# Attention outputs of a two-layer hybrid decoder as float32r products of split values and split, already divided probabilities, on one Trainium2 core

## Chip, cores and metric

One core of a Trainium2 chip (trn2) runs the whole kernel in one launch. The metric is the device time of an execution in microseconds, as the median of three runs. PE is TensorE, DVE is VectorE, ACT is ScalarE, POOL is GpSimd, SP is SyncE, which issues nearly all DMAs.

## What is computed

Two layers, each a half-step SwiGLU, a token-mixing sub-layer and another half-step SwiGLU, all on 512 tokens of width 1024, in float32. The mixing has three parts side by side: forgetting attention (4 heads of 64), dilated attention (4 heads of 64) and an HGRN2 recurrence (4 heads of 128). The part at hand is the two attentions:

```
def _fox_attention(q, k, v, c):
...
        s = jnp.einsum('bhqd,bhkd->bhqk', qi, k).astype(jnp.float32) * scale
        s = s + ci[..., None] - c[:, :, None, :]
...
        p = jax.nn.softmax(jnp.where(mask, s, NEG_BIG), axis=-1)
        return jnp.einsum('bhqk,bhkd->bhqd', p.astype(v.dtype), v)
...
def _dilated_attention(q, k, v):
    outs, lses = [], []
    for window, dilation in DILATED_PATTERNS:
        o, lse = _dilated_branch(q, k, v, window, dilation)
        outs.append(o)
        lses.append(lse)
    wts = jax.nn.softmax(jnp.stack(lses, 0), axis=0)
    return jnp.sum(wts[..., None] * jnp.stack(outs, 0), axis=0)
...
    o = jnp.concatenate([oa.astype(h.dtype), ob.astype(h.dtype), oc.astype(h.dtype)], axis=-1)
    return o @ w_out
```

The kernel computes the three dilated patterns as one softmax: the logarithm of the number of patterns that hold a pair of positions is added to its score by a mask. The sum over the patterns weighted by their denominators is just that softmax.

## The kernel before

Activations stand transposed, as [column, token], in eight blocks of 128 columns by 512 tokens. Large products run in float32r, one pass over PE, on operands that are split in two: a float32r high part that ACT casts (L269 for the weights) and the low part, which DVE gets by subtraction (L271). A product is then three matmuls, high by high, high by low and low by high (mm3, L274 to L278). Weights come by DMA in 512 KB pieces, three ahead (L266).

`ffn` and the closures of `mixing` are written as plain loops. The instructions of each engine stand in an order that the build decides from dependencies and priorities: `load_split` raises the priority of the weights' splits by 400 places (AHEAD), `run` that of the chains of the mixing by 100 (CHAIN). At run time each engine takes its list in that order.

In `mixing` come, for each layer: the HGRN heads (`decays`, `states`), the dilated attention, the forgetting attention, and `gated`, which projects the gate (`proj_t("HG")`, into hg_ps), applies a sigmoid (L840), multiplies the HGRN outputs by it and transposes them. While that goes on, `first_rows` starts the output projection (o_ps). `add_rows` takes the row blocks in the order f, d, h: two of forgetting attention (ohf and olf, the high and low parts of its transposed output), two of dilated (ohd, old), four of HGRN.

`attend` (L637 to L673) does both attentions, for four blocks of 128 queries (b) and four heads (h). For one head and n = 128(b + 1) keys:

- PE writes the scores into the one bank sc (L647), from float32r operands.
- DVE adds the mask and takes the minimum of the negated scores, into neg and nm (L651).
- ACT takes the exponential in place and sums it into den (L655).
- PE transposes the 128x128 pieces into the one bank pt (L659).
- ACT, for odd heads, or DVE, for even heads, copies them to pt in memory (L662, L664).
- PE multiplies in plain float32, the transposed probabilities being the stationary operand and the 64 columns of values the moving one (L666), into po as [query, column]:

```
                        PE.matmul(po[:, h * HD:(h + 1) * HD], pt[:, j * 128:(j + 1) * 128],
                                  val[:, j, h * HD:(h + 1) * HD], start=j == 0, stop=j == b)
```

Behind the four heads DVE divides by den (L669 and L671, into o), and `put_out` transposes the two pieces of o on PE (L537), ACT casts the high part (L542), and DVE subtracts for the low one (L543). The values vv are one plain float32 tile of [128, 4, 512], which ACT writes out of v_ps (L724).

Of the kernel before, what the change touches and what calls it, by code (L numbers as in the profile page):

```python
# [19 lines left out]
HD = 64  # L20
# [109 lines left out]
def hybrid_trunk(ctx: ExitStack, tc: tile.TileContext, a, out):  # L130
# [355 lines left out]
    def mixing(l, after, r, rb):  # L486
# [150 lines left out]
        def attend(kind, operands, val, mask):  # L637

            for b in range(NB):
                n = (b + 1) * 128  # L640
                den = lines(mp, [128, 4], tag="den", name="den", bufs=2)
                po = gen("po", "po")
                for h in range(4):
                    ps = gen("sc", "sc_ps")
                    terms = operands(h)
                    for i, (q, k) in enumerate(terms):
                        PE.matmul(ps[:, 0:n], q[:, b * 128:(b + 1) * 128], k[:, 0:n],  # L647
                                  start=i == 0, stop=i == len(terms) - 1)
                    neg = mp.tile([128, T], F32, tag="neg", name="neg", bufs=3)
                    nm = lines(mp, [128, 1], tag="nm", name="nm", bufs=2)  # L650
                    V.tensor_tensor_reduce(out=neg[:, 0:n], in0=ps[:, 0:n], in1=mask[:, 512 - n:512],  # L651
                                           scale=-1.0, scalar=3.0e38, op0=ALU.add, op1=ALU.min,
                                           accum_out=nm)
                    pr = neg
                    S.activation(pr[:, 0:n], neg[:, 0:n], AF.Exp, bias=nm, scale=-1.0,  # L655
                                 accum_out=den[:, h:h + 1])
                    pt_ps = gen("pt", "pt_ps")
                    for j in range(b + 1):
                        PE.transpose(pt_ps[:, j * 128:(j + 1) * 128], pr[:, j * 128:(j + 1) * 128], ident)  # L659
                    pt = mp.tile([128, T], F32, tag="pt", name="pt", bufs=2)  # L660
                    if h % 2:
                        S.copy(pt[:, 0:n], pt_ps[:, 0:n])  # L662
                    else:
                        V.tensor_copy(pt[:, 0:n], pt_ps[:, 0:n])  # L664
                    for j in range(b + 1):
                        PE.matmul(po[:, h * HD:(h + 1) * HD], pt[:, j * 128:(j + 1) * 128],  # L666
                                  val[:, j, h * HD:(h + 1) * HD], start=j == 0, stop=j == b)
                    yield
                V.reciprocal(den, den)  # L669
                o = mp.tile([128, 4, HD], F32, tag="o4", name="o4", bufs=1)  # L670
                V.tensor_tensor(out=o, in0=po[:, 0:256].rearrange("p (h d) -> p h d", h=4),  # L671
                                in1=den.unsqueeze(2).to_broadcast([128, 4, HD]), op=ALU.mult)
                put_out(kind, b, o.rearrange("p h d -> p (h d)"), 2)  # L673


        vv = slot("VV", (128, NB, 512), "vv")


        def dilated():
# [41 lines left out]
                                               op0=ALU.mult, op1=ALU.subtract)  # L721
            pss = proj_t("V", "v_ps")
            for b in range(NB):
                S.activation(vv[:, b, :], pss[b], AF.Copy, scale=r[:, b:b + 1])  # L724
            dv = vv[:, :, 0:256]
            def operands(h):
                i, n = divmod(h, 2)
                return [(q2[i][:, n, :], kh[i][:, n, :]), (q2[i][:, n, :], kl[i][:, n, :])]
# [20 lines left out]
            return ch, cl  # L749

        def forgetting(ch, cl):
            fv = vv[:, :, 256:512]


            q2 = [pair(t, f"fq{t}", R32) for t in ("A2", "A6")]
            k2 = [pair(t, f"fk{t}", R32) for t in ("V0", "V1")]
            qc = [pair(t, f"fqc{t}", R32) for t in ("am", "F0")]
            kc = [pair(t, f"fkc{t}", R32) for t in ("F1",)]
            kc.append(slot("ob", (128, 3, T), "fkcob", R32)[:, 0:2, :])
            for i in range(2):  # L760
                G.memset(qc[i][64:68].bitcast(F32), -1.0)
                G.memset(kc[i][64:68].bitcast(F32), 1.0)
                for n in range(2):
                    h = 2 * i + n
                    for part, c in enumerate((ch, cl)):
                        nc.sync.dma_start(out=qc[i][66 + part:67 + part, n, :].bitcast(F32), in_=c[h:h + 1, :].bitcast(F32))
                        nc.sync.dma_start(out=kc[i][64 + part:65 + part, n, :].bitcast(F32), in_=c[h:h + 1, :].bitcast(F32))
                ps = proj_d(f"FQ{i}", "fq_ps")
                u = mp.tile([128, 768], F32, tag="qk", name="fu", bufs=2)[:, 0:T]
                V.scalar_tensor_tensor(out=u, in0=ps, scalar=0.125, in1=rb, op0=ALU.mult, op1=ALU.mult)  # L770
                for n in range(2):
                    own, other = slice(64 * n, 64 * n + 64), slice(64 - 64 * n, 128 - 64 * n)
                    S.copy(q2[i][own, n, :], u[own])
                    S.copy(qc[i][0:64, n, :], u[own])
                    V.tensor_tensor(out=q2[i][other, n, :], in0=u[own], in1=q2[i][own, n, :].bitcast(F32),
                                    op=ALU.subtract)
                ps = proj_d(f"FK{i}", "fk_ps")
                u = mp.tile([128, 768], F32, tag="qk", name="fu", bufs=2)[:, 0:T]
                V.tensor_tensor(out=u, in0=ps, in1=rb, op=ALU.mult)
                for n in range(2):  # L780
                    own, other = slice(64 * n, 64 * n + 64), slice(64 - 64 * n, 128 - 64 * n)
                    S.copy(k2[i][own, n, :], u[own])
                    S.copy(k2[i][other, n, :], u[own])
                    V.tensor_tensor(out=kc[i][0:64, n, :], in0=u[own], in1=k2[i][own, n, :].bitcast(F32),
                                    op=ALU.subtract)
            def operands(h):
                i, n = divmod(h, 2)
                return [(q2[i][:, n, :], k2[i][:, n, :]), (qc[i][0:68, n, :], kc[i][0:68, n, :])]

            return attend("f", operands, fv, masks[:, 0, :])  # L790


# [78 lines left out]
        def add_rows(half, pair):  # L871
            wh, wl = load_split(a["w_out"][l, half, pair], KB, 128)
            for i in range(2):
                d = 2 * pair + i
                if not half:
                    pss[d] = acc("o_ps")
                for j in range(4):
                    k = 4 * half + j
                    kind, n = rows[k]
                    mm3(pss[d], wh[:, 4 * i + j, :], wl[:, 4 * i + j, :], oth[kind][n // 2][:, n % 2, :],  # L880
                        otl[kind][n // 2][:, n % 2, :], k == 0, k == KB - 1)
                if half:
                    V.tensor_tensor(out=x[d], in0=pss[d], in1=x[d], op=ALU.add)
                    after(d)
                yield
# [53 lines left out]
```

## Time and profile before

| | us |
|---|---|
| median of three runs | 2067.0 (2066.81 to 2067.48) |
| profiled execution | 2066.05 |
| its span, from the first to the last instruction | 2064.3 |
| PE busy | 2043.4 (99%) |
| DVE busy | 1025.8 (50%) |
| ACT busy | 731.6 (35%) |
| granted TensorE clock, mean | 0.999 |

PE is occupied throughout. Its matmuls are pipelined, so the duration of one (0.39 us for 512 columns) is longer than the step from one to the next. A plain float32 matmul leaves two records, a float32r matmul and a transpose one. The attention stands in two stretches, at 511 to 621 us and, for the second layer, about 1562 to 1641 us.

### The profile page before, as it was taken

How to read it: one execution, taken by the hardware profiler on the slowest of the kernel's cores; microseconds unless marked ns; L12 is line 12 of the kernel's file. 1: busy time of each engine (PE TensorE's matmuls, PEld its weight loads, DVE VectorE, ACT ScalarE, POOL GpSimd, SP SyncE). 2: the span in 40 equal slices, each digit the busy share in tenths (PEclk: the TensorE clock that was granted, in tenths of full speed). 3: DMA queues.
4: the chain of work that ended last, by engine and by line, in shares of the span. 5: the costliest groups of instructions: out<-in, count | busy, mean ns of one | idle time of the engine just before them, and what ended most of it. 6: DMA issues, size and time to landing. Idle time of an engine off the chain costs nothing.

```text
span 2064.3 us, 23885 instructions
## 1 busy us (share of the span) xinstructions
PE 2043.4 (99%) x9636; PEld 1685.6 (82%) x9636; DVE 1025.8 (50%) x1636; ACT 731.6 (35%) x1104; POOL 12.8 (1%) x18
## 2 busy tenths in 40 slices
PE   8999999999999999999999999999999999999998
PEld 6888888888788888888888888888888888888886
DVE  8544433556656644443354444336566565444333
ACT  5332322433654323232232322233346443232222
POOL 0000000000000000000000000000000000000000
PEclk9999999999999999999999999999999999999999
DMA  4323233211212232333323233332112122323222
GB/s 169 97 97 100 91 95 104 93 52 61 67 42 92 92 96 98 98 92 98 101 92 102 92 102 94 95 97 82 62 42 77 52 92 93 102 92 102 97 97 82
DMA packets 54310, 184.91 MB, mean 90 GB/s; under 512 B 7336, under 2 KB 7464, under 8 KB 54200
## 3 DMA queue, kind: packets, MB, share of 16 engines
q1 hardware_dynamic: 53592, 182.28, 27.6%
q8 instruction: 75, 1.23, 0.2%
q10 hardware_dynamic: 576, 1.05, 0.1%
q14 instruction: 35, 0.29, 0.0%
q0 software_dynamic: 32, 0.07, 0.0%
HBM read 181.21 MB, written 2.10 MB: 89 GB/s over the span
## 4 chain that ended last, share of the span: by engine, by line
PE 95%; DVE 2%; ACT 1%; issue 1%; DMA 0%; SPq 0%; DVEq 0%; ACTq 0%
PE gu_ps L278 15%; PE gu_ps L277 15%; PE gu_ps L276 15%; PE d_ps L276 6%; PE d_ps L278 6%; PE d_ps L277 6%; PE d_ps L451 5%; PE lv_ps L593 2%; PE po L666 2%; PE o_ps L278 1%; PE o_ps L276 1%; PE o_ps L277 1%; PE sc_ps L647 1%; PE pt_ps L659 1%; PE hg_ps L517 1%; PE hg_ps L518 1%
## 5 line engine op out<-in xcount | busy, mean ns | idle before, releaser
L269 ACT CAST wh<-raw 128x1024 fp32r<-128x1024 f32 (+1 forms) x344 | 357.2, 1039 | 1053.9 <-issue 407.8
L271 DVE TENSOR_TENSOR wl<-raw,wh 128x1024 fp32r<-128x1024 f32 (+1 forms) x344 | 414.2, 1205 | 300.4 <-ACT wh L269 298.4
L276 PE MATMUL gu_ps<-xh,wh 128*128 128x512 f32 x1408 | 548.6, 390 | 6.6 <-ACT wh L269 6.6
L278 PE MATMUL gu_ps<-xh,wl 128*128 128x512 f32 x1408 | 548.8, 390 | 0.2
L277 PE MATMUL gu_ps<-xl,wh 128*128 128x512 f32 x1408 | 548.2, 389 | 0.0
L276 PEld LDWEIGHTS gu_ps<-xh,wh 128*128 128x128 f32 x1408 | 264.7, 188 | 61.6 <-ACT wh L269 6.6
L278 PEld LDWEIGHTS gu_ps<-xh,wl 128*128 128x128 f32 x1408 | 264.6, 188 | 56.2 <-DVE wl L271 1.3
L277 PEld LDWEIGHTS gu_ps<-xl,wh 128*128 128x128 f32 x1408 | 264.7, 188 | 55.2 <-DVE xl L190 0.2
L276 PE MATMUL d_ps<-hh,wh 128*128 128x512 f32 x528 | 205.4, 389 | 0.0
L277 PE MATMUL d_ps<-hl,wh 128*128 128x512 f32 x528 | 205.4, 389 | 0.0
L278 PE MATMUL d_ps<-hh,wl 128*128 128x512 f32 x528 | 205.4, 389 | 0.0
L406 DVE TENSOR_TENSOR u<-gu_ps,rb 128x512 f32<-128x512 f32 x88 | 60.8, 691 | 265.1 <-PE gu_ps L278 264.9
L403 DVE TENSOR_TENSOR g<-gu_ps,rb 128x512 f32<-128x512 f32 x88 | 60.8, 691 | 172.9 <-PE gu_ps L278 172.7
L278 PEld LDWEIGHTS d_ps<-hh,wl 128*128 128x128 f32 x528 | 99.1, 188 | 20.6
L277 PEld LDWEIGHTS d_ps<-hl,wh 128*128 128x128 f32 x528 | 99.1, 188 | 20.6
L276 PEld LDWEIGHTS d_ps<-hh,wh 128*128 128x128 f32 x528 | 99.1, 188 | 20.5
L409 ACT CAST hh<-u 128x512 fp32r<-128x512 f32 x88 | 55.1, 626 | 57.5 <-DVE u L407 57.5
L451 PE MATMUL d_ps<-wl,hh 128*128 128x512 f32 x176 | 69.0, 392 | 0.3 <-DVE wl L271 0.3
L451 PE MATMUL d_ps<-wh,hl 128*128 128x512 f32 x176 | 68.8, 391 | 0.0
L451 PE MATMUL d_ps<-wh,hh 128*128 128x512 f32 x176 | 68.4, 392 | 0.0
L407 DVE TENSOR_TENSOR u<-u,g 128x512 f32<-128x512 f32 x88 | 60.9, 692 | 8.1
L593 PEld LDWEIGHTS lv_ps<-hQ,hk 128*128 128x128 f32 x448 | 55.7, 191 | 8.4 <-issue 6.1
(292 smaller groups left out, 2403.3 us busy)
## 6 DMA issues: line engine op xcount, KB each, us to landing
raw<-in_ffn_w_gate SPq DMA_DIRECT2D x88, 512.0 KB, 3.4
raw<-in_ffn_w_up SPq DMA_DIRECT2D x88, 512.0 KB, 3.4
raw<-in_w_in SPq DMA_DIRECT2D x58, 512.0 KB, 3.4
raw<-in_ffn_w_down SPq DMA_DIRECT2D x48, 448.0 KB, 3.3
raw<-in_ffn_w_down SPq DMA_DIRECT2D x24, 512.0 KB, 3.5
raw<-in_last_w_down SPq DMA_DIRECT2D x22, 512.0 KB, 3.5
raw<-in_w_out SPq DMA_DIRECT2D x16, 512.0 KB, 3.4
x<-in_x SPq DMA_DIRECT2D x8, 256.0 KB, 5.4
```

What stands on the lines that cost most here:

```text
L269: S.copy(wh, raw)
L271: V.tensor_tensor(out=wl, in0=raw, in1=wh.bitcast(F32), op=ALU.subtract)
L276: PE.matmul(ps, lh, rh, start=first, stop=False)
L277: PE.matmul(ps, lh, rl, start=False, stop=False)
L278: PE.matmul(ps, ll, rh, start=False, stop=last)
L403: V.tensor_tensor(out=g, in0=part[0], in1=rb, op=ALU.mult)
L406: V.tensor_tensor(out=u, in0=part[1], in1=rb, op=ALU.mult)
L407: V.tensor_tensor(out=u, in0=u, in1=g, op=ALU.mult)
L409: S.copy(h1, u)
L451: PE.matmul(ps, h[:, s], w, start=first and n == 0, stop=last and n == len(terms) - 1)
L593: PE.matmul(ps[:, e:e + 64], K[:, hh, s], Q[:, hh, s].rearrange("p (n two c) -> p n two c", two=2, c=c)[:, :, 1, :], start=True, stop=True)
L666: PE.matmul(po[:, h * HD:(h + 1) * HD], pt[:, j * 128:(j + 1) * 128], val[:, j, h * HD:(h + 1) * HD], start=j == 0, stop=j == b)
```

## The change

The values vv become float32r and hold a high and a low part for each head, side by side, 128 columns in all. Each head divides its probabilities before it transposes them: a reciprocal of its own column of den, and a scaling of neg, on ACT for odd heads and on DVE for even ones. The transposed probabilities are split: ph is a float32r cast on ACT, pl the rest on DVE. For each 128 keys two float32r matmuls follow, with the 128 columns of split values as the stationary operand and ph and then pl as the moving one, so that po holds, for each head, [column, query]: the products with the high parts in partitions 0 to 63, those with the low parts in 64 to 127. Behind the four heads ACT copies the lower half to low, DVE adds it to the upper one (two instructions, into u), ACT casts the high part and DVE subtracts for the low one. The transposes of `put_out` go for the two attentions. neg has two buffers, not three. Two tiles of the forgetting attention move from slots of their own (F0, F1) to those of HGRN heads (A1, A4). In the first half of the output projection the dilated rows come ahead of the others.

```
-                    neg = mp.tile([128, T], F32, tag="neg", name="neg", bufs=3)
+                    neg = mp.tile([128, T], F32, tag="neg", name="neg", bufs=2)
...
+                    V.reciprocal(den[:, h:h + 1], den[:, h:h + 1])
+                    if h % 2:
+                        S.activation(pr[:, 0:n], pr[:, 0:n], AF.Copy, scale=den[:, h:h + 1])
+                    else:
+                        V.tensor_scalar(out=pr[:, 0:n], in0=pr[:, 0:n], scalar1=den[:, h:h + 1], scalar2=None,
+                                        op0=ALU.mult)
                     pt_ps = gen("pt", "pt_ps")
                     for j in range(b + 1):
                         PE.transpose(pt_ps[:, j * 128:(j + 1) * 128], pr[:, j * 128:(j + 1) * 128], ident)
-                    pt = mp.tile([128, T], F32, tag="pt", name="pt", bufs=2)
-                    if h % 2:
-                        S.copy(pt[:, 0:n], pt_ps[:, 0:n])
-                    else:
-                        V.tensor_copy(pt[:, 0:n], pt_ps[:, 0:n])
+                    ph = mp.tile([128, T], R32, tag="ph", name="ph", bufs=2)
+                    S.copy(ph[:, 0:n], pt_ps[:, 0:n])
+                    pl = mp.tile([128, T], R32, tag="pl", name="pl", bufs=1)
+                    V.tensor_tensor(out=pl[:, 0:n], in0=pt_ps[:, 0:n], in1=ph[:, 0:n].bitcast(F32),
+                                    op=ALU.subtract)
+                    hs = slice(h * 128, (h + 1) * 128)
                     for j in range(b + 1):
-                        PE.matmul(po[:, h * HD:(h + 1) * HD], pt[:, j * 128:(j + 1) * 128],
-                                  val[:, j, h * HD:(h + 1) * HD], start=j == 0, stop=j == b)
+                        js = slice(j * 128, (j + 1) * 128)
+                        PE.matmul(po[:, hs], val[:, j, h].rearrange("p n d -> p (n d)"), ph[:, js],
+                                  start=j == 0, stop=False)
+                        PE.matmul(po[:, hs], val[:, j, h].rearrange("p n d -> p (n d)"), pl[:, js],
+                                  start=False, stop=j == b)
                     yield
-                V.reciprocal(den, den)
-                o = mp.tile([128, 4, HD], F32, tag="o4", name="o4", bufs=1)
-                V.tensor_tensor(out=o, in0=po[:, 0:256].rearrange("p (h d) -> p h d", h=4),
-                                in1=den.unsqueeze(2).to_broadcast([128, 4, HD]), op=ALU.mult)
-                put_out(kind, b, o.rearrange("p h d -> p (h d)"), 2)
...
+                pv = po.rearrange("p (i n t) -> p i n t", i=2, n=2)
+                low = small.tile([128, 2, 2, 128], F32, tag="sq", name="low")[0:64]
+                S.copy(low, pv[64:128])
+                u = mp.tile([128, 2, 128], F32, tag="o4", name="o4", bufs=1)
+                for n in range(2):
+                    V.tensor_tensor(out=u[64 * n:64 * n + 64], in0=pv[0:64, :, n, :], in1=low[:, :, n, :], op=ALU.add)
+                bs = slice(b * 128, (b + 1) * 128)
+                hi, lo = oth[kind][0][:, :, bs], otl[kind][0][:, :, bs]
+                S.copy(hi, u)
+                V.tensor_tensor(out=lo, in0=u, in1=hi.bitcast(F32), op=ALU.subtract)
...
-        vv = slot("VV", (128, NB, 512), "vv")
+        vv = slot("VV", (128, NB, 8, 2, HD), "vv", R32)
...
-                S.activation(vv[:, b, :], pss[b], AF.Copy, scale=r[:, b:b + 1])
-            dv = vv[:, :, 0:256]
+                pv = pss[b].rearrange("p (h d) -> p h d", h=8)
+                S.activation(vv[:, b, :, 0, :], pv, AF.Copy, scale=r[:, b:b + 1])
+                V.scalar_tensor_tensor(out=vv[:, b, :, 1, :], in0=pv, scalar=r[:, b:b + 1],
+                                       in1=vv[:, b, :, 0, :].bitcast(F32), op0=ALU.mult, op1=ALU.subtract)
+            dv = vv[:, :, 0:4]
...
-            qc = [pair(t, f"fqc{t}", R32) for t in ("am", "F0")]
-            kc = [pair(t, f"fkc{t}", R32) for t in ("F1",)]
+            qc = [pair(t, f"fqc{t}", R32) for t in ("am", "A1")]
+            kc = [pair(t, f"fkc{t}", R32) for t in ("A4",)]
...
-                for j in range(4):
+                for j in range(4) if half else (2, 3, 0, 1):
...
-                        otl[kind][n // 2][:, n % 2, :], k == 0, k == KB - 1)
+                        otl[kind][n // 2][:, n % 2, :], k == 2, k == KB - 1)
```

The build moves instructions beyond that. Two places show it; L859 is the sigmoid of the gate in the changed kernel (L840 before), L667 the cast ph, L659 the scaling on ACT, L682 the copy low, L688 the cast hi, L674 and L676 the products with ph and pl.

ACT at the end of the first layer's forgetting attention, before, from the copy of the last head's transposed probabilities on:

```order
L662 COPY pt<-pt_ps 128x512
L269 CAST wh<-raw 128x1024
L542 CAST ohf<-ot_ps 128x2x128
L840 ACT_TABLE_LOAD
L840 ACTIVATE gate<-hg_ps_4635,rs_r 128x512
L840 ACTIVATE gate<-hg_ps_4636,rs_r 128x512
L269 CAST wh<-raw 128x1024
L840 ACTIVATE gate<-hg_ps_4637,rs_r 128x512
L269 CAST wh<-raw 128x1024
L840 ACTIVATE gate<-hg_ps_4638,rs_r 128x512
```

The same place with the change, from the first gate to the second of the last block's exponentials (the other two, two more gates and three more table loads follow in the same manner):

```order
L682 COPY low<-po 64x512
L859 ACT_TABLE_LOAD
L859 ACTIVATE gate<-hg_ps_4839,rs_r 128x512
L688 CAST ohf<-o_4715 128x2x128
L655 ACT_TABLE_LOAD
L655 ACTIVATE neg,den<-neg,nm 128x512
L859 ACT_TABLE_LOAD
L859 ACTIVATE gate<-hg_ps_4840,rs_r 128x512
L269 CAST wh<-raw 128x1024
L667 CAST ph<-pt_ps 128x512
L655 ACT_TABLE_LOAD
L655 ACTIVATE neg,den<-neg,nm 128x512 x2
```

What moved: the gates stood behind the whole attention, with one table load; now the four of them stand between the exponentials of its last block, with seven.

PE in that last block, before (from the third head's products on):

```order
L666 MATMUL po<-vv,pt 128x64 x4
L659 MATMUL pt_ps<-ident,neg 128x128 x4
L516 MATMUL hg_ps_4638<-wh,xh_2453 128x512
L517 MATMUL hg_ps_4638<-wl,xh_2453 128x512
L518 MATMUL hg_ps_4638<-wh,xl_2455 128x512
L516 MATMUL hg_ps_4635<-wh,xh_2546 128x512
L666 MATMUL po<-vv,pt 128x64 x4
L517 MATMUL hg_ps_4635<-wl,xh_2546 128x512
L518 MATMUL hg_ps_4635<-wh,xl_2548 128x512
L516 MATMUL hg_ps_4635<-wh,xh_2639 128x512
L537 MATMUL ot_ps<-ident,o_4622 128x128
```

With the change, from the middle of the last head's products on:

```order
L537 MATMUL ot_ps<-ident,ho_2682 128x128
L676 MATMUL po<-pl,vv 128x128
L537 MATMUL ot_ps<-ident,ho_2682 128x128
L674 MATMUL po<-ph,vv 128x128
L537 MATMUL ot_ps<-ident,ho_2682 128x128
L676 MATMUL po<-pl,vv 128x128
L537 MATMUL ot_ps<-ident,ho_2682 128x128
L674 MATMUL po<-ph,vv 128x128
L676 MATMUL po<-pl,vv 128x128
L537 MATMUL ot_ps<-ident,ho_2683 128x128 x4
L276 MATMUL o_ps<-ohf,wh 128x512 x2
L277 MATMUL o_ps<-olf,wh 128x512
```

What moved: before, 23 matmuls of the gate's projection stood behind the last product; now the projection is over before the block's second head, the dilated rows of o_ps are used between its heads, and four transposes alone stand between the last product and the first matmul that needs ohf.

## Rows read from the trace of the kernel before

**Rows 1.** The page: span, busy time of the engines, chain that ended last by engine

```profile
span 2064.3 us, 23885 instructions
...
PE 2043.4 (99%) x9636; PEld 1685.6 (82%) x9636; DVE 1025.8 (50%) x1636; ACT 731.6 (35%) x1104; POOL 12.8 (1%) x18
...
PE 95%; DVE 2%; ACT 1%; issue 1%; DMA 0%; SPq 0%; DVEq 0%; ACTq 0%
```

**Rows 2.** Busy time by stretch: us, then each engine's, clock, DMA share, GB/s

```profile
541.00:625.00 84.00, 83.88 (x501) 68.20 (x501) 47.93 (x122) 49.01 (x110) 0.00 (x0) 1.00 0.16 51
1565.00:1645.00 80.00, 79.95 (x481) 65.47 (x481) 45.60 (x115) 45.44 (x104) 0.00 (x0) 1.00 0.16 51
```

**Rows 3.** Timeline of PE, 618 to 626 us: start, us, engine, line, operation, tiles

```profile
618.87 1.07 PE L666 MATMUL po<-vv,pt 128*128 128x64 f32 x8
...
622.14 0.39 PE L517 MATMUL hg_ps<-wl,xh 128*128 128x512 f32 x1
...
625.31 0.39 PE L276 MATMUL o_ps<-ohf,wh 128*128 128x512 f32 x1
```

**Rows 4.** Timeline of ACT, 612 to 627 us

```profile
614.49 0.72 ACT L655 ACTIVATE neg<-neg,nm 128x512 f32<-128x512 f32 x1 [0.32 <-DVE nm L651]
615.12 0.19 ACT L655 ACTIVATION_READ_ACCUMULATOR neg<-neg,nm 128x1 f32 x1
...
621.58 1.28 ACT L840 ACT_TABLE_LOAD   x1
622.87 0.69 ACT L840 ACTIVATE gate<-hg_ps,rs_r 128x512 f32<-128x512 f32 x1
625.56 0.69 ACT L840 ACTIVATE gate<-hg_ps,rs_r 128x512 f32<-128x512 f32 x1 [2.00 <-PE hg_ps L518]
```

**Rows 5.** Timeline of PE's weight loads, 607 to 611 us and 513 to 514 us

```profile
607.59 0.64 PEld L666 LDWEIGHTS po<-vv,pt 128*128 128x128 f32 x5
...
610.49 0.43 PEld L659 LDWEIGHTS pt_ps<-ident,neg 128*128 128x128 f32 x4 [0.20 <-DVE olf L543]
...
513.45 0.19 PEld L647 LDWEIGHTS sc_ps<-dkhA,dqB 128*128 128x128 f32 x1
513.56 0.19 PEld L647 LDWEIGHTS sc_ps<-dklA,dqB 128*128 128x128 f32 x1
```

**Rows 6.** ACT's groups, 541 to 625 us: count, busy us, mean ns, idle before

```profile
L655 ACT ACTIVATE neg<-neg,nm 128x256 f32<-128x256 f32 (+3 forms) x29 | 16.9, 582 | 12.1 <-DVE nm L651 12.0
L269 ACT CAST wh<-raw 128x1024 fp32r<-128x1024 f32 x8 | 8.4, 1047 | 3.9 <-PE fk_ps L277 2.7 <-PE hg_ps L518 0.7 <-PE fq_ps L277 0.4
L662 ACT COPY pt<-pt_ps 128x128 f32<-128x128 f32 (+3 forms) x16 | 6.8, 425 | 11.0 <-PE pt_ps L659 10.3 <-PE sc_ps L647 0.4
...
L773 ACT CAST fqA<-fu 64x512 fp32r<-64x512 f32 x4 | 2.5, 620 | 0.0
...
L542 ACT CAST ohf<-ot_ps 128x256 fp32r<-128x256 f32 x4 | 1.5, 374 | 4.2 <-PE ot_ps L537 4.2
```

**Rows 7.** Groups of instructions by shape, whole span

```profile
L188 ACT ACTIVATE xh<-x,par 128x512 fp32r<-128x512 f32 x48 | 34.3, 724 | 20.6 <-DVE x L883 20.5
...
L662 ACT COPY pt<-pt_ps 128x512 f32<-128x512 f32 x8 | 4.7, 588 | 12.6 <-PE pt_ps L659 12.0 <-PE sc_ps L647 0.6
...
L567 DVE TENSOR_SCALAR hk<-hk,lba 128x512 f32<-128x512 f32 x8 | 3.5, 483 | 0.0
```

**Rows 8.** DVE's groups, 541 to 625 us

```profile
L664 DVE COPY pt<-pt_ps 128x128 f32<-128x128 f32 (+3 forms) x16 | 7.8, 490 | 6.9 <-PE pt_ps L659 6.7
L671 DVE TENSOR_TENSOR o<-po,den 128x256 f32<-128x256 f32 x8 | 3.4, 424 | 7.6 <-PE po L666 7.6
...
L669 DVE RECIPROCAL den<-den 128x4 f32<-128x4 f32 x8 | 1.4, 175 | 2.7 <-ACT neg L655 2.7
```

**Rows 9.** Timeline of SP's DMA issues, 500 to 545 us

```profile
504.68 0.33 SPq L266 DMA_DIRECT2D raw<-in_w_in  x1
524.69 0.50 SPq L767 DMA_DIRECT2D fkcob<-ch  x1
```

More of the change, by code (lines that the diff above doesn't have):

```diff
@@ L751, in forgetting @@
         def forgetting(ch, cl):
-            fv = vv[:, :, 256:512]
+            fv = vv[:, :, 4:8]
             q2 = [pair(t, f"fq{t}", R32) for t in ("A2", "A6")]
             k2 = [pair(t, f"fk{t}", R32) for t in ("V0", "V1")]
-            qc = [pair(t, f"fqc{t}", R32) for t in ("am", "F0")]
-            kc = [pair(t, f"fkc{t}", R32) for t in ("F1",)]
+            qc = [pair(t, f"fqc{t}", R32) for t in ("am", "A1")]
+            kc = [pair(t, f"fkc{t}", R32) for t in ("A4",)]
             kc.append(slot("ob", (128, 3, T), "fkcob", R32)[:, 0:2, :])
```

## Prediction

> **What bounds the kernel now.** First the page: PE is busy for 2043.4 us of a span of 2064.3 us, and the chain that ended last runs on PE for 95% of it [rows 1]. So a change counts in two ways only: by the time that PE's own instructions take, and by the time that PE has to stand still for another engine. The profiled execution took 2066.05 us, 1.75 us more than its span and 0.95 us less than the 2067.0 us median of the runs; the sum below is made against 2066.05 us. About 0.2% (4.1 us) is what a measurement of this kernel can tell from no change.
>
> Next the two stretches that the change touches, one for each layer, from the first transposed probabilities to the first products of the output projection [rows 2]. PE is busy 83.88 of 84 us and 79.95 of 80 us, at a granted clock of 1.00, while DVE works 47.93 and 45.60 us and ACT 49.01 and 45.44 us. The reader is to see that ACT and DVE have about 35 us to spare in each layer, and PE nothing.
>
> Then the end of the stretch. The last eight products of the last block go at 618.87, then PE goes on with the gate projection (hg_ps), at 622.14 among others, and at 625.31 with the first product on ohf [rows 3]; the 14 matmuls from 622.14 to 625.31 stand 0.226 us apart, the pace of every 512-column matmul here. Nothing waits: the attention was over 5 us before its result was needed. ACT meanwhile loads its table for the sigmoid once, at 621.58, and runs the gates at 622.87 and 625.56 [rows 4].
>
> **PE's own instructions.** A plain float32 product of attention (128x64) leaves two records on PE, and five loads of its kind take 0.64 us, which is 0.11 us each [rows 5]. So 80 products of a layer are 160 records of 0.11 us, 17.9 us. Now they are 160 float32r products of 128 columns, whose nearest relatives are the 128-column scores: two loads at 513.45 and 513.56, again 0.11 us apart [rows 5]. So the new products cost what the old ones did. The bounds are far apart: a quarter of the 0.226 us of 512 columns, 0.06 us, if the columns alone count, and those 0.226 us; I take 0.11, since that row is of the same form. What PE does save is the transposes of the output: 16 in a layer at 0.11 us (four loads in 0.43 us [rows 5]), 1.8 us.
>
> **ACT.** In a layer it loses 16 copies (6.8 us) and 8 casts of 0.37 us (3.0 us) [rows 6]. It gains 32 casts ph at the copies' mean of 0.425 us (13.6 us); 16 scalings, which no row shows, between the copy, 0.588 us for 512 columns, and an activation with a scale from memory, 0.724 us [rows 7], of which I take the copies' mean and 0.1 us (8.4 us), nearer to the second, since it has the same operands; 8 copies low at 0.588 us (4.7 us) and 8 casts hi at 0.37 us (3.0 us). Together +19.9 us. And it loads tables six times more: the built order has seven loads at the end where there was one, 1.28 us each [rows 4], +7.7 us. So ACT goes from 49 to some 77 us in a stretch of 82.
>
> **DVE.** It loses 16 copies (7.8 us), 8 divisions (3.4 us) and 8 reciprocals (1.4 us) [rows 8]. It gains 32 subtractions pl at the copies' mean of 0.49 us (15.7 us), 16 scalings (0.483 us for 512 columns [rows 7], 0.35 as a mean by ACT's ratio of 0.425 to 0.588; 5.6 us), 32 reciprocals (5.6 us), 16 sums at 0.424 us (6.8 us) and 4 low parts of the values, at most twice 0.424 us (3.4 us): +24.5 us, so 72 of 82 us. Neither engine is over PE as a mean. The places decide.
>
> **The end of the stretch.** The order puts the gate projection ahead of the last block of forgetting attention, and the sigmoids of the gates between its exponentials. From the end of hg_ps's first column block to the first product on ohf, ACT has this, in this order and by the rows: 7 table loads (9.0 us), 4 gates of 0.69 (2.8), 4 exponentials of 0.82 with their sums (614.49 to 615.31; 3.3) [rows 4], 4 casts ph of 0.588 (2.4), 2 scalings of 0.7 (1.4), 1 weight cast of 1.05, 3 casts of 0.37 (1.1): 21.0 us. In two places it must wait, about 1 us together: for the reciprocal on DVE ahead of head 1's scaling, and for PE's transposes ahead of the last ph. Behind the last ph stand pl (0.69), seven more products and their latency (1.0), low (0.59), two sums (0.85) and hi (0.37), 3.5 us: 25.5 us in all. PE has for that time 18 matmuls of hg_ps and 24 of o_ps (42 x 0.226 = 9.5), 8 scores (1.8), 16 transposes (1.8), 32 products (3.5) and 16 transposes of the HGRN outputs (1.8): 18.4 us. So PE stands still for **7 us a layer**. Bounds: 5 (no waits, and ACT's instructions overlapping by some 0.05 us each) and 12 (0.2 us more at each of some 25 hand-overs, where one in the row of 614.49 left ACT idle for 0.32 [rows 4]).
>
> The Trainium skill, ScalarE: Activation LUTs, section Table sets, says to batch activations by their set, not by function. This order does the opposite, and the trace of before, with its one load ahead of four gates, keeps the rule; no run here shows yet what breaking it costs.
>
> **The beginning of the stretch.** From the first transposes to the last product of the third block, PE has 61 projection matmuls (13.8), 48 products (5.4), 24 transposes (2.6) and 22 scores (3.5), 25.4 us. ACT has 12 ph (4.5), 12 exponentials (8.0: a mean of 0.58 and 0.19 for the sum, less the 0.1 by which they overlap), 12 casts of 64x512 at 0.62 (7.4) and 3 weight casts of 1.05 (3.2) [rows 6], 5 scalings (2.6), 3 low (1.8), 2 hi (0.7) and one table load (1.3): 29.5 us. ACT is short by **4 us a layer**, and later blocks, where more gate and key projections stand between, do not add to that. Bounds: 0, if part of ACT's list is done before PE gets there, and 9: for every second head the exponential on ACT, the reciprocal on DVE (0.175 us [rows 8]) and the scaling on ACT follow each other, with 0.32 us at each hand-over [rows 4] 0.8 us, and six such heads put 5 us on top.
>
> The third buffer of neg that goes costs nothing beside this: scores wait for the one bank sc_ps anyway. Eight small DMAs a layer move, with their tiles, to slots that the HGRN heads free before the attention; SP sends nothing between 504.68 and 524.69 [rows 9], so they fit there. The projection's new order (dilated rows first) moves only which products stand behind the last hi, and is in the 18.4 us above.
>
> **The sum.** For a layer -1.8 + 7 + 4 = +9.2 us, twice +18.4: 2066.05 + 18.4 = 2084.5 us, and at the median 0.95 us more, **2085 us**. The forecast's own bounds (5 to 9 and 1 to 6) give 2075 to 2094.
>
> **Rivals.**
> (a) Not slower. If the table loads ran in ACT's idle time, the end would be free: ACT's list there without loads is 12 us, with its 1 us of waits and the 3.5 us behind 16.5 us, against PE's 18.4. The point from which it decides is a load that holds ACT for under 0.3 us; with the start covered too, the transposes remain: 2 x -1.8, 2063.5 us, at most 2068 with some waits. For it: ACT's spare 35 us. Against it: exponentials and gates alternate in one queue, and in row 621.58 the load takes its full 1.28 us with the gate right behind it.
> (b) ACT and DVE in lock-step all along. Then the first three blocks lose 9 us (above) and the end 9, with 0.8 us for each of its two second heads: -1.8 + 9 + 9 = +16.2 a layer, 2098.5 us at the profile and 2099.5 at the median; 2094 to 2105 with fewer such waits or more. For it: both engines near 90% and in each other's chain for every head. Against it: the order keeps projection work between most heads.
> (c) A dearer switch of tables. If each of the six more loads a layer held ACT for twice its 1.28 us, since the engine would have to run empty as well, the end would lose 7.7 us more, in all 2 x (9.2 + 7.7) = +33.8 us: 2100 at the profile, 2101 us at the median. Against it: the load of 621.58 ends at 622.86, and the gate starts at 622.87 [rows 4].
> The Trainium skill, ScalarE: Activation LUTs, section What ACT_TABLE_LOAD costs, states 1283 ns for the load and some 1380 ns of drain with every switch; an estimate by that page is 8.3 us more a layer and 2102 us. The trace agrees with the load's duration and shows no drain behind it.
> (d) The products are cheaper than the scores: at 0.06 us each they would give back 2 x 160 x 0.05 = 16 us, and 2069 us come out. Against it stands the row of the scores.
>
> **Chances.** Forecast 57%, (a) 11%, (b) 25%, (c) 5%, (d) 2%. The range reaches from 2071 to 2104 us: it leaves out (a), (d) and the far ends of (b) and of the forecast. Of (a), 3 points lie more than 0.2% below 2067.0 and 8 within 0.2%, as do the 2 of (d); the rest is slower: 0.03, 0.10, 0.87.
>
> **What would show it.** Right: the new po products 0.11 us apart; 12 table loads more than before, seven between the first gate and the last ph of each layer; PE's loads waiting for ph and pl in the last block for several us; DVE and ACT some 25 us busier in each stretch. Wrong: PE without gaps while the gates run (a); waits for ph, pl or neg spread evenly over all eight blocks (b); idle ACT behind each load (c). A time under 2071 us would refute the sum at the end of the stretch.

## Result and profile after

| | before | after |
|---|---|---|
| median, us | 2066.9 | 2098.8 |
| profiled execution, us | 2066.05 | 2098.47 |
| its span, us | 2064.3 | 2096.7 |
| last matmul of the output projection, layer 0 / layer 1, us | 670.5 / 1690.2 | 685.8 / 1722.0 |

By the medians of four runs each (one more of the kernel before than above) the changed kernel takes 31.9 us more, where 18 were forecast. The ratio of all runs is 1.016 (interval 1.0147 to 1.0172): three runs of the changed kernel took 2098.5 to 2098.9 us and one 2103.3. Layer 0 gives 15.3 us of it (685.8 less 670.5), layer 1 gives 16.5.

The page after, beside [rows 1]:

```profile
span 2096.7 us, 24034 instructions
...
PE 2058.2 (98%) x9604; PEld 1686.9 (80%) x9604; DVE 1068.9 (51%) x1772; ACT 782.3 (37%) x1196; POOL 12.9 (1%) x18
...
PE 90%; ACT 5%; DVE 4%; issue 1%; DMA 0%; SPq 0%; ACTq 0%; DVEq 0%
```

PE has 32 records fewer, the transposes of two layers. ACT has 50.7 us more, DVE 43.1, and together they now have 9% of the chain that ended last, where they had 3%. Busy time by stretch, to be read against [rows 2] (columns as there; the first stretch begins with the first transposed probabilities, the second with the gate projection, the third with the first gate):

```profile
545.20:585.70 40.50, 38.85 (x213) 29.03 (x214) 30.94 (x84) 32.02 (x71) 0.00 (x0) 1.00 0.15 51
585.70:623.00 37.30, 35.66 (x193) 26.68 (x192) 24.17 (x75) 24.98 (x61) 0.00 (x0) 1.00 0.13 43
623.00:648.00 25.00, 20.59 (x111) 16.82 (x110) 18.74 (x50) 21.33 (x35) 0.00 (x0) 0.93 0.13 43
```

No stretch is full any more. The third is the forecast's end of the stretch: ACT busy 21.33 of 25 us, PE 20.59, at a granted clock of 0.93. ACT's timeline there, beside [rows 4]:

```profile
621.91 1.28 ACT L859 ACT_TABLE_LOAD   x1
623.21 0.69 ACT L859 ACTIVATE gate<-hg_ps,rs_r 128x512 f32<-128x512 f32 x1
...
633.21 1.28 ACT L859 ACT_TABLE_LOAD   x1
634.50 0.69 ACT L859 ACTIVATE gate<-hg_ps,rs_r 128x512 f32<-128x512 f32 x1
...
635.68 1.28 ACT L655 ACT_TABLE_LOAD   x1
```

Seven such loads stand between 621.91 and 639.11, gates and exponentials in turn. Each gate starts 0.01 to 0.02 us behind its load. PE's timeline beside it (start, us, engine, line, operation, tiles; in brackets the idle time before and what ended it):

```profile
631.77 0.28 PE L674 MATMUL po<-ph,vv 128*128 128x128 f32 x1
631.88 0.27 PE L676 MATMUL po<-pl,vv 128*128 128x128 f32 x1
632.00 0.27 PE L674 MATMUL po<-ph,vv 128*128 128x128 f32 x1
...
633.25 0.66 PE L665 MATMUL pt_ps<-ident,neg 128*128 128x128 f32 x4 [0.50 <-ACT neg L659]
635.24 0.61 PE L276 MATMUL o_ps<-ohd,wh 128*128 128x512 f32 x1 [1.34 <-ACT gate L859]
635.65 0.63 PE L277 MATMUL o_ps<-old,wh 128*128 128x512 f32 x1
636.08 0.63 PE L278 MATMUL o_ps<-ohd,wl 128*128 128x512 f32 x1
```

The new products stand 0.11 us apart, as forecast. The row of 635.24 is one that the forecast lacked: the output projection, which was to be PE's work while ACT was late, itself waits for a gate, because hg_ps holds the four banks that it needs until the gates have read them.

Earlier in the layer PE waits too. Waits of PE's weight loads up to the first gate (total us, times, longest), after the change, in the first three blocks of the dilated attention (545.2 to 575.2 us) and behind them (to 623 us):

```profile
PEld po L674 <- ACT ph L667: 3.9, 10, 0.8
PEld po L676 <- DVE pl L669: 1.4, 7, 0.2
PEld sc_ps L647 <- DVE nm L651: 1.4, 4, 0.8
...
PEld po L674 <- ACT ph L667: 5.0, 11, 1.0
PEld po L676 <- DVE pl L669: 2.7, 10, 0.4
PEld sc_ps L647 <- DVE nm L651: 2.3, 7, 0.8
```

and before it, in the first three blocks (541 to 565.9 us) and behind them (to 625 us, the last block included):

```profile
PEld po L666 <- ACT pt L662: 0.9, 3, 0.4
PEld sc_ps L647 <- DVE nm L651: 0.5, 2, 0.3
PEld po L666 <- DVE pt L664: 0.5, 3, 0.2
...
PEld po L666 <- ACT pt L662: 1.9, 6, 0.5
PEld po L666 <- DVE pt L664: 1.5, 6, 0.3
PEld ot_ps L537 <- DVE o L671: 0.8, 4, 0.2
PEld sc_ps L647 <- DVE nm L651: 0.8, 2, 0.4
```

By these rows (smaller ones, 2.2 us after and 1.8 before, are left out) the waits are 16.7 us where they were 6.9. Of the 9.8 us more, 4.8 lie in the first three blocks (6.7, before 1.9) and 5.0 behind them (10.0, before 5.0). A load's wait need not be PE's loss: before, with 6.9 us of them, PE was busy for 83.88 of 84 us. The medians of e8 below give the loss itself.

### The profile page after: what moved, and what is told of

Read it like the earlier page. It is cut to its first block, busy times and chain, and to the rows that moved or that the text cites. A ratio compares the mean times of both kernels' runs of the same rounds, so it can differ in the third digit from the quotient of the medians.

```text
span 2096.7 us, 24034 instructions
## 1 busy us (share of the span) xinstructions
PE 2058.2 (98%) x9604; PEld 1686.9 (80%) x9604; DVE 1068.9 (51%) x1772; ACT 782.3 (37%) x1196; POOL 12.9 (1%) x18
## 4 chain that ended last, share of the span: by engine, by line
PE 90%; ACT 5%; DVE 4%; issue 1%; DMA 0%; SPq 0%; ACTq 0%; DVEq 0%
PE gu_ps L276 15%; PE gu_ps L278 15%; PE gu_ps L277 15%; PE d_ps L278 6%; PE d_ps L276 6%; PE d_ps L277 6%; PE d_ps L451 5%; PE lv_ps L593 2%; PE o_ps L277 1%; PE o_ps L278 1%; PE o_ps L276 1%; ACT wh L269 1%; PE ho_ps L839 1%; ACT neg L655 1%; PE hf_ps L278 1%
```

## Experiments

Medians, with ratios to the kernel before from runs on the same chip:

| kernel | median, us | ratio (interval) |
|---|---|---|
| change, as given | 2098.8 | 1.0160 (1.0147 to 1.0172) |
| e1 tanh gates | 2107.0 | 1.0196 (1.0179 to 1.0213) |
| e2 second bank for transposes | 2101.5 | 1.0168 (1.0152 to 1.0183) |
| e4 tanh gates, no division | 2100.8 | 1.0165 (1.0150 to 1.0180) |
| e5 tanh gates, same addresses | 2090.4 | 1.0115 (1.0100 to 1.0130) |
| e6 e5 without low parts | 2094.4 | 1.0134 (1.0117 to 1.0151) |
| e7 e5 with a third head in flight | 2097.5 | 1.0147 (1.0132 to 1.0162) |
| e8 e5 with gates behind the attention | 2082.8 | 1.0077 (1.0062 to 1.0092) |
| e9 before, side edits alone | 2065.8 | 0.9996 (0.9987 to 1.0004) |
| e10 before, division in heads alone | 2078.1 | 1.0056 (1.0042 to 1.0069) |
| e11 change, old row order | 2115.7 | 1.0235 (1.0219 to 1.0251) |
| e12 e8, dilated attention first too | 2080.5 | 1.0066 (1.0052 to 1.0079) |

**e1, e5: the table loads.**

```
-            V.tensor_scalar(out=ss, in0=ss, scalar1=1.0 / 128, scalar2=EPS, op0=ALU.mult, op1=ALU.add)
+            V.tensor_scalar(out=ss, in0=ss, scalar1=4.0 / 128, scalar2=4 * EPS, op0=ALU.mult, op1=ALU.add)
...
+            rh = lines(small, [128, NB], tag="rh", name="rh")
+            V.tensor_scalar(out=rh, in0=r, scalar1=0.5, scalar2=None, op0=ALU.mult)
...
-                S.activation(gate, pss[b], AF.Sigmoid, scale=r[:, b:b + 1])
-                V.tensor_tensor(out=gate, in0=gate, in1=nw, op=ALU.mult)
+                S.activation(gate, pss[b], AF.Tanh, scale=rh[:, b:b + 1])
+                V.scalar_tensor_tensor(out=gate, in0=gate, scalar=1.0, in1=nw, op0=ALU.add, op1=ALU.mult)
```

> The gates' sigmoid is computed as 0.5 + 0.5 tanh(x/2), with tanh where the exponential's table already holds it, so that the gates and the exponentials can stand mixed without table loads; the factor 0.5 goes into the normalisation's constants. Theory A (the seven table loads of each layer, 9.0 us of ACT's time, are what PE stands still for at the end of the stretch): PE's 7.6 us a layer of lost time there falls to 0 to 2, and the lower granted clock there goes with it: 2083 to 2088 us. Rival (the end is set by the order itself: gates ahead of the last exponentials, which hold the banks that the output projection needs, and by hand-overs): it falls by under 3 us a layer: 2093 to 2099 us.

It measured 2107.0 us, 8 us above the change, so neither theory held. The same kernel ran once more as e3, as a companion of e4, and took 2105.2 us. The page showed where: 14 table loads fewer, ACT 17.6 us less busy, but PE 11.0 us more (2069.2), with as many matmuls. The down projections of the feed-forward layers, which the edit does not touch, had become slower. In e1's timeline 18 steps take 4.20 us, 0.233 each:

```profile
959.73 0.39 PE L276 MATMUL d_ps<-hh,wh 128*128 128x512 f32 x1
...
963.93 0.39 PE L276 MATMUL d_ps<-hh,wh 128*128 128x512 f32 x1
```

The tile rh (64 bytes a partition, two buffers) had moved every tile behind it by 128 bytes. e5 takes them back out of a padding tile:

```
-PAD = 96
+PAD = 64
```

> The tanh gates again, with the padding tile in front of the later pools smaller by 128 bytes a partition, which is what the tile of halved row factors had moved them by. Theory A2 (in the first tanh kernel half of the d_ps products outside the mixing stood 240 ns apart instead of 227, 13 us in all, because the tiles behind had moved by 128 bytes; the tables themselves give 3 us a layer): all d_ps products are 227 ns apart again, 2091 to 2095 us. Rival (the slower d_ps products come from something else, such as the order): 2103 to 2107 us again.

2090.4 us, just below A2's interval, and the same 18 steps take 4.09 us, 0.227 each:

```profile
959.75 0.39 PE L276 MATMUL d_ps<-hh,wh 128*128 128x512 f32 x1
...
963.84 0.39 PE L276 MATMUL d_ps<-hh,wh 128*128 128x512 f32 x1
```

The addresses cost 16.6 us (2107.0 less 2090.4). Without the table loads the change is 8.4 us faster (2098.8 less 2090.4), 4.2 a layer. The end of the stretch in e5 runs at the full granted clock:

```profile
626.60:645.00 18.40, 15.76 (x94) 11.86 (x93) 14.94 (x39) 11.75 (x25) 0.00 (x0) 1.00 0.10 30
```

So the 8.4 us hold what the lower clock had cost. By the granted clocks of the change (0.93 at the end of both layers, and 0.66 for 5 us more in layer 1, shown in the last section) that is an estimated 5 us. ACT is busy 11.75 of 18.40 us in e5 and still PE is not full. PE waits for no gate any more. Its longest wait is for the sums behind the last head's products (L685), when PE has no other work left:

```profile
644.25 0.63 PE L537 MATMUL ot_ps<-ident,ho 128*128 128x128 f32 x4 [1.70 <-DVE o L685]
```

The loads, with the clock, are about half of what the end costs.

**e8: the order at the end**, on top of e5.

```
-        run(f)
+        with tc.high_priority(600):
+            for _ in f:
+                pass
```

> Tanh gates, same addresses, and the forgetting attention at priority 600 instead of 100, so that most of its last block stands ahead of the gate projection's end and of the gates. Theory E (at the end PE stands still because the gates, and with them the banks for the output projection, stand in the same queue as the last exponentials; with the projection as cover behind the last products it would not): the 5 us a layer that PE loses from the last gate product on fall to 1 to 2, 6 to 8 us under the tanh gates alone. Rival (the gate projection is then used up as cover elsewhere, and the last head's chain stands bare): within 3 us of the tanh gates alone.

2082.8 us, 7.6 below e5: theory E. PE's timeline at the end of e8 has no idle time in it from 632.05 us on:

```profile
632.77 0.28 PE L676 MATMUL po<-pl,vv 128*128 128x128 f32 x1
632.88 0.45 PE L517 MATMUL hg_ps<-wl,xh 128*128 128x512 f32 x1
...
635.72 0.50 PE L276 MATMUL o_ps<-ohf,wh 128*128 128x512 f32 x1
```

As in [rows 3], gate projection and output projection stand between the last product and the first matmul on ohf. Loads and order together are 16.0 us (2098.8 less 2082.8), **8.0 us a layer**, and this is nearly the whole of the end, since PE is full behind 632.05 us. What e8 still loses to before, 15.9 us, lies ahead of that, in the heads.

**e11: the row order undone.**

```
-                for j in range(4) if half else (2, 3, 0, 1):
+                for j in range(4):
...
-                        otl[kind][n // 2][:, n % 2, :], k == 2, k == KB - 1)
+                        otl[kind][n // 2][:, n % 2, :], k == 0, k == KB - 1)
```

> The changed kernel with the output projection's first half in the old order again, forgetting rows first. Theory H (the dilated rows that come first are cover for the last head's chain: three matmuls for each of two row blocks and four column blocks, 24 in all at 0.226 us): undone, PE stands still for 4 to 6 us a layer more, 2106 to 2111 us. Rival (the projection waits for the gates' banks anyway, so the order of its rows tells nothing): 2096 to 2101 us.

2115.7 us, 8.5 us a layer worse than the change. Theory H had the sign, and its 24 matmuls are 5.4 us of it. PE stood idle longer (15.40 of 24 us busy), and its granted clock was lower, 0.66 where the change has 0.93 at about the same place:

```profile
626.00:650.00 24.00, 15.40 (x74) 12.52 (x72) 15.96 (x41) 18.42 (x31) 0.00 (x0) 0.66 0.06 22
```

**e9, e10: two parts of the change alone, in the kernel before.** e9 has two buffers of neg and the moved slots:

```
-                    neg = mp.tile([128, T], F32, tag="neg", name="neg", bufs=3)
+                    neg = mp.tile([128, T], F32, tag="neg", name="neg", bufs=2)
...
-            qc = [pair(t, f"fqc{t}", R32) for t in ("am", "F0")]
-            kc = [pair(t, f"fkc{t}", R32) for t in ("F1",)]
+            qc = [pair(t, f"fqc{t}", R32) for t in ("am", "A1")]
+            kc = [pair(t, f"fkc{t}", R32) for t in ("A4",)]
```

> The kernel before with two of the change's side edits alone: two buffers of neg instead of three, and the two tiles of the forgetting attention in the slots of HGRN heads. As the prediction said, they cost nothing: 2065 to 2069 us. Rival (the third buffer let the scores of a head run ahead, and its loss is part of what the first seven blocks lose): 2 to 4 us a layer, 2071 to 2075 us.

No difference, 0.9996. e10 has the division in each head:

```
+                    V.reciprocal(den[:, h:h + 1], den[:, h:h + 1])
+                    if h % 2:
+                        S.activation(pr[:, 0:n], pr[:, 0:n], AF.Copy, scale=den[:, h:h + 1])
+                    else:
+                        V.tensor_scalar(out=pr[:, 0:n], in0=pr[:, 0:n], scalar1=den[:, h:h + 1], scalar2=None,
+                                        op0=ALU.mult)
...
-                V.reciprocal(den, den)
...
-                V.tensor_tensor(out=o, in0=po[:, 0:256].rearrange("p (h d) -> p h d", h=4),
-                                in1=den.unsqueeze(2).to_broadcast([128, 4, HD]), op=ALU.mult)
+                V.tensor_copy(o, po[:, 0:256].rearrange("p (h d) -> p h d", h=4))
```

> The kernel before with one part of the change alone: each head divides its probabilities before it transposes them (a reciprocal of 0.16 us on DVE, and a scaling of 0.55 us on ACT or 0.38 us on DVE), and the division behind the four heads becomes a copy. Products, copies and the transposes of the outputs stay. Theory G (each hand-over more in a head's chain costs PE time, because PE's order has the products and scores just behind the instructions that they wait for, although ACT and DVE have 35 us a layer to spare): 2 to 4 us a layer, 2071 to 2075 us. Rival (it hides beside PE, and only the end and ACT's long list count): 2066 to 2068 us.

2078.1 us, 11.4 more than before: more than theory G said, and in another place. The first two stretches are as full as before, with ACT and DVE nearly as busy as in the change; the loss is in the third:

```profile
542.50:583.50 41.00, 41.00 (x251) 33.97 (x251) 29.61 (x82) 30.78 (x69) 0.00 (x0) 1.00 0.17 53
583.50:622.80 39.30, 39.16 (x230) 32.27 (x229) 25.05 (x74) 27.54 (x56) 0.00 (x0) 1.00 0.17 54
622.80:632.00 9.20, 5.60 (x32) 4.72 (x31) 5.97 (x16) 5.88 (x11) 0.00 (x0) 0.75 0.18 60
```

ACT's timeline says why: with the division in the heads the build put gates ahead of the last exponentials, with a load for each change.

```profile
616.66 1.28 ACT L655 ACT_TABLE_LOAD   x1
617.96 0.72 ACT L655 ACTIVATE neg<-neg,nm 128x512 f32<-128x512 f32 x1
...
619.73 1.28 ACT L844 ACT_TABLE_LOAD   x1
621.03 0.69 ACT L844 ACTIVATE gate<-hg_ps,rs_r 128x512 f32<-128x512 f32 x1
```

So the division alone, in the kernel before, brings a loss of the same kind at the end (5.7 us a layer, where the change has 8.0), and none in the seven blocks.

**e2, e4, e6, e7, e12: the seven blocks.** e2 gives the transposes of odd heads a bank of their own:

```
-                    pt_ps = gen("pt", "pt_ps")
+                    pt_ps = gen("lv" if h % 2 else "pt", "pt_ps")
```

> The transposed probabilities of odd heads go to the bank that the HGRN levels have left (lv), those of even heads to pt as before, so PE can transpose a head before the products of the one ahead of it are through. Theory B (in the first seven blocks PE stands still because each head is a chain of hand-overs through single banks, 8 us a layer over what it was): 3 to 8 us a layer come back, 2083 to 2093 us, and the waits for ph get fewer. Rival (ACT simply has too much to do there): the list of ACT is the same, so 2096 to 2100 us, and the waits for ph move elsewhere.

2101.5 us: nothing gained, and just above the rival's interval. Its waits for ph fell from 8.9 to 4.4 us in layer 0, and loads of transposes now waited for the scaling (3.8 us, against 0.6 in the change). e4 leaves lines L657 to L662 out; e3, beside it, is e1's kernel:

> Beside the next kernel on the same chip: the tanh gates alone, for a trace on the same chip. 2083 to 2088 us if the table loads are the cause of the end's loss, 2093 to 2099 us if not.

> The tanh gates, and the division of the probabilities left out (reciprocals and scalings: the outputs of the attentions are not divided by their denominators), so it is read against the tanh gates alone. A layer loses 16 scalings of 0.55 us on ACT and 16 of 0.38 us and 32 reciprocals of 0.16 us on DVE. Theory C (the division, which stands in each head's chain between exponential and transposes, is what slows the first seven blocks): 5 to 8 us a layer faster than the tanh gates alone, 10 to 16 us in all. Rival (the casts ph and subtractions pl alone set the pace): 0 to 3 us a layer, 0 to 6 us in all.

2100.8 us, 6.2 below e1, the kernel with the same addresses: 3.1 us a layer, about the rival's upper bound. PE's loads still waited for ph (7.4 us) and pl (3.5) in layer 0. e6, on e5, has no low part:

```
-                    V.tensor_tensor(out=pl[:, 0:n], in0=pt_ps[:, 0:n], in1=ph[:, 0:n].bitcast(F32),
-                                    op=ALU.subtract)
+                    pl = ph
```

> Tanh gates, same addresses, and the low part of the probabilities left out: no subtraction on DVE, and the second product of each pair takes the high part again, so PE's work is the same and one hand-over in each head's chain goes, with 0.5 us of DVE for each head. Theory D (in the first seven blocks PE waits for the chain of a head, exponential, reciprocal, scaling, transposes, cast, subtraction, of which only two heads are in flight, and the order leaves too little projection work as cover): 4 to 8 us a layer come back, 8 to 16 us under the tanh gates alone. Rival (what counts is ACT's list, which stays as it is): 0 to 4 us in all.

2094.4 us, 4 us slower than e5 with 0.5 us of DVE less for each head. Neither theory allowed for that. Addresses are not the reason: the down projections step 0.227 us here, and in e7. The waits for pl are gone, and those for ph are 10.3 us (545.7 to 631.8 us):

```profile
PEld po L672 <- ACT ph L667: 10.3, 20, 1.3
```

e7 makes room for a third head (pl in a dead tile, three buffers of neg, e2's bank):

```
+                    neg = mp.tile([128, T], F32, tag="neg", name="neg", bufs=3)
+                    pt_ps = gen("lv" if h % 2 else "pt", "pt_ps")
+                    pl = slot("qx", (128, T), "pl", R32)
```

> Tanh gates, same addresses, and room for a third head in flight: neg has three buffers again (the low part takes the place of a dead HGRN tile), and the transposes of odd heads use the bank of the HGRN levels. No engine gets less to do. Theory D: 3 to 8 us a layer come back in the first seven blocks, 6 to 16 us under the tanh gates alone. Rival (the buffers cost nothing, as the prediction said): within 3 us of the tanh gates alone.

2097.5 us, 7 us slower than e5; some 2 us of that is a lower granted clock, 0.85 from 1600 to 1614 us, in the second layer alone. Theory D falls twice: neither a shorter chain nor more heads in flight gave anything back. Each build sets the order anew, and in e7 the waits for ph fell to 3.3 us (8.7 in e5) while those for pl rose to 5.9 (4.2). That the order is the cause is not shown, since no run kept it fixed. e12 runs the dilated attention at priority 200 on top of e8:

> The best version so far (tanh gates, same addresses, forgetting attention at priority 600) with the dilated attention at priority 200 instead of 100. Theory G: the order within the heads stays, so what the first seven blocks lose over before stays at 8 to 10 us a layer, and the time at 2079 to 2084 us, slower than before. Rival (the loss is the priority's doing, with projections and weight casts ahead of the dilated heads): 2070 to 2076 us.

2080.5 us, within theory G's interval, though e10 has taken its reason away. This is the best version of the change that was found, and it is still 0.66% slower than the kernel before.

One late head shows what such a wait is made of. ACT's timeline in e8:

```profile
575.13 0.73 ACT L655 ACTIVATE neg<-neg,nm 128x512 f32<-128x512 f32 x1 [0.45 <-DVE nm L651]
...
575.97 0.58 ACT L682 COPY low<-po 64x512 f32<-64x512 f32 x1
576.58 0.59 ACT L667 CAST ph<-pt_ps 128x512 fp32r<-128x512 f32 x1
```

and PE's:

```profile
574.70 0.62 PE L665 MATMUL pt_ps<-ident,neg 128*128 128x128 f32 x4
...
577.58 0.30 PE L674 MATMUL po<-ph,vv 128*128 128x128 f32 x1 [0.60 <-DVE o L685]
```

The transposes are done at 575.32 (574.70 and 0.62). The cast ph starts 1.26 us later, because the next head's exponential and the copy low of the block before are ahead of it in ACT's queue. It is done at 577.17. The product waits longer still, for the two sums (L685) that must have read the bank po and that come behind low. PE has five projection matmuls and two scores to put between, and then 0.60 us of nothing.

## Why the prediction came out as it did

The sign was right and 2098.8 lies in the range (2071 to 2104), but of 31.9 us the sum explained 18. It lies outside the sum's own bounds (2075 to 2094), which were narrower than the bounds of its two steps; the range held it because rival (b) had widened it. By its steps, for a layer:

- **PE's own instructions, -1.8 us: right.** Products 0.11 us apart at 631.77, 631.88 and 632.00, 32 records fewer.
- **ACT and DVE: right.** Forecast 27.6 us more on ACT with the loads, 24.5 on DVE; the page has 25.4 (half of 50.7) and 21.6.
- **The end, 7 us: 8.0 measured** (e8). The seven loads are there, and from the first of them (621.91) to the first product on ohf (647.79) it is 25.9 us, where the sum had 25.5. But the parts are not the sum's. Without loads it would have had the end free (16.5 us of ACT's list and waits against 18.4 of PE's work), and e5 still loses 3.8 us: PE has used up its other work when the last head's products are through (row 644.25), and e8, which keeps some for that place, is free of this wait. The other half, 4.2 us, goes with the loads, but it holds two terms that the sum did not have: o_ps, which it counted as PE's work, is held back by the gates' banks (row 635.24), and the clock is lower. Neither is so in e5.
- **The beginning, 4 us: right in size for the three blocks it was made for.** From the first transposes to the last product of the third block it took 29.7 us, where the sum had 29.5 of ACT's list against 25.4 of PE's work:

```profile
545.19 0.30 PE L665 MATMUL pt_ps<-ident,neg 128*128 128x128 f32 x1
...
574.92 0.28 PE L676 MATMUL po<-pl,vv 128*128 128x128 f32 x1
```

  This was luck in part: ACT was busy for 25.66 of these 29.7 us, since its instructions overlap (their times add up to 28.9), so it was not short as a sum. It had room, and PE waited all the same.
- **The later blocks, nothing: the step that failed.** The prediction said that they "do not add to that". The loads' waits there grew from 5.0 to 10.0 us, as much as in the first three. The medians agree: with 8.0 for the end and -1.8, 31.9 us (16.0 a layer) leave 9.8 a layer for all seven blocks, and 4 of these had been forecast. The step compared ACT's sum with PE's over a whole stretch. PE waits at a head whose cast, or low and sums, stand too far back in ACT's queue, though ACT is idle for 11.6 us before other casts ph of the same layer. A mean over a stretch cannot show this.
- **Buffers and slots, nothing: right** (e9). **The row order**, which the prediction booked in the end's cover, is worth 8.5 us a layer (e11), more than its 5.4 us of matmuls.

Rival (b), with 2099.5 us, hit the time and its sign, waits spread over all blocks, but by luck. It had 9 us in the first three blocks, where the waits grew by 4.8, 9 at the end and nothing between, and it put the loss on the division's hand-overs in second heads. e10 has those hand-overs and loses nothing before the end; e4 is without them and only 3.1 us a layer faster. Rival (a) is out: each load held ACT for its full 1.28 us. So is (c): the gate at 623.21 starts with the load's end at 623.19. The Trainium skill, ScalarE: Activation LUTs, section What ACT_TABLE_LOAD costs, adds a drain of some 1380 ns to each switch; no load in this trace shows one (the gate of 623.21 comes 0.02 us behind its load). The section Table sets, which says to batch by set, is borne out by e5: gates by tanh, with no loads between them and the exponentials, give 8.4 us back, the clock's share included. (d) is out by the products' spacing.

What stays open is which part of the split itself makes the seven blocks lose 9.8 us: the cast ph on ACT for every head, where before ACT and DVE took turns; the bank po, which is now held until low and both sums have read it; or the order that a build makes of them. These three were not tried apart. The bank's direct share is small: in the change PE's products waited 1.2 us for the sums in both layers together. Division (e10, e4), low parts (e6), buffers and banks (e7, e2, e9) are excluded as the sole cause, as far as runs can tell whose order changed with each edit.

## What to carry to other kernels

Where PE is full and other engines have room, do not price an added instruction by the room of its engine over a stretch, but by what stands ahead of it in that engine's queue when PE comes for its result. Longer heads can also move other work, here gates in front of exponentials: look in the built order for every place where two table sets or two holders of a bank become mixed, and price what is taken as cover by its own waits. Keep an experiment's addresses where they were before its time is read.

## What was not expected of the hardware

- **The granted clock.** In the kernel before it is 1.00 in the stretches of both layers [rows 2]. After the change PE stood idle for 0.50 us ahead of 633.25 and 1.34 us ahead of 635.24, and then:

```profile
635.20:638.60 3.40, 3.36 (x11) 2.78 (x11) 2.50 (x7) 3.35 (x5) 0.00 (x0) 0.54 0.00 0
```

That is about 1.2 of 2.4 GHz for 3.4 us; matmuls of 512 columns begin 0.43 us apart (635.65 and 636.08) instead of 0.227, so some 1.6 us are lost on top of the idle time. In the 6.4 us behind that stretch it stood at 0.98 again. In layer 1 it fell once more, behind 1.87 us of idle time:

```profile
1682.00:1687.00 5.00, 4.99 (x17) 4.02 (x18) 1.60 (x4) 1.39 (x4) 0.00 (x0) 0.66 0.01 3
```

In layer 0 it stayed at 1.00 behind the same idle time (1.86 us ahead of 647.41). The 1.7 us that this costs (5 us at 0.66) are enough for the 1.2 us that layer 1 loses more than layer 0 (16.5 less 15.3). Why the two layers differ is open.

- **Addresses.** Moving tiles by 128 bytes a partition made one group of matmuls step 0.233 us instead of 0.227, with the same instructions and operands. Over the 2112 matmuls of the down projections that is some 13 of the 16.6 us between e1 and e5, more than the table loads cost; the output projection's steps were longer too (0.232 us in e1, 0.227 in e5). Which operand's address it is was not tried.
- **Less work, slower.** e6 took 0.5 us of DVE and one hand-over out of every head and lost 4 us. Its order was another one; that this is the reason is not shown.
